# Low weights of the opening's features made on GpSimd instead of VectorE, and the first roots spread half a feature later

## The chip, the cores and the metric

The kernel runs on one core of a Trainium2 chip. The metric is the device time of one execution in microseconds (us), as the median of several runs; smaller is better. The engines are TensorE (PE in the profile), VectorE (DVE), ScalarE (ACT), GpSimd (POOL) and SyncE (SP, which here issues nearly all DMAs).

## The reference

One layer of a bidirectional encoder is applied to two groups of tokens, 2048 (prompt) and 512 (sample), each with the same 16 meta tokens ahead of them. All numbers are float32.

```python
u = rms_norm(h, norm_g)
proj = u @ w_in                                   # 1024 x 5376
qa, ka, va, za, qb, kb, vb, zb, ga, gb = jnp.split(proj, cuts, axis=-1)
o_a = neighbourhood_attention(qa, ka, va, na_rpb, n)      # 8 heads, 2-D windows
o_b = window_attention(qb, kb, vb, t5_bias, sink, n)      # 8 query heads, 2 key heads
y_a = (o_a * silu(za)) @ w_proj_a
y_b = (o_b * silu(zb)) @ w_proj_b
merged = sigmoid(ga) * y_a + sigmoid(gb) * y_b
out = rms_norm(h + merged @ w_out, final_g)               # meta tokens dropped
```

## The kernel before

The 2560 tokens are cut into five blocks of 512; the last block also carries the 16 meta tokens. The 5376 output columns of `w_in` are cut into 42 features of 128. Products are kept at float32 quality by splitting each operand into a high part (a cast, `fp32r`) and a low part (the rest): `project` computes a feature with `mm3`, three matmuls (L146: high weight by high input, L147: high by low, L148: low by high) for each of the 8 slices of the 1024 inputs, 24 matmuls of 512 columns in all. Key and value features of the last block are made in two column pieces, of 256 and of 272 columns, with 48 shorter matmuls.

`split_w` makes the two parts of one feature's weights, a tile `wt`, out of the raw tile `wraw` that a DMA brought. It works in two halves of 512 columns; each is a cast on ScalarE (L207) and a subtraction `l = r - h` (L208), on the engine that is handed in, or else on `lo_eng[0]`, which is VectorE until late in the program. There are two buffers each for `wraw` and `wt`: the cast of a feature's weights waits until TensorE has done the feature two before it, and the next raw DMA waits until a raw tile is split.

The change is in the opening, the first stage. `beside` computes 18 features of the last block (four of QA, four of QB, four of KA, four of VA, KB and VB), one after the other by `alone`, while the operands of blocks 0 and 1 are prepared by the steps of `prep_first` (L377 scaling, L445 to L461 sums and differences, L381 casts and L382 low parts). The roots of the last block's norm come from the generator `own` (`prep_last`): at the count `own[1][0]` of quarter features its sums run on TensorE (L360) and its reciprocal roots on VectorE (L153 to L163, and L177, which writes them on diagonals, `rs_dg`); at the last count of `own[1]` the roots are spread over the partitions by matmuls with ones (L185) and copied by ScalarE (L370). Until then the finished features wait in PSUM (`held[1]`), since their stores (L281: PSUM times root) need the roots.

After the 18 features comes the opening's exit. `begin` computes the first two products of blocks 0 and 1 (`pa`, `pc`, L850), and `sides_first` makes sums of the raw weights on VectorE (L816, L817, L821, L823: tiles `s`), which are split into the operands of the next products: `x2` (a tile `wt` made from `s`, used by the product called p6, `pa`, and by p5, `pe`) and `x3`, `x4` (used by p7 and later). `last_operands` makes eight more block operands at the same place (L381, L382). From there on TensorE goes through pairs of features.

TensorE and SyncE run in the order in which the code is written. The order of the other engines is set by a scheduler from its own estimates, so an edit can move their instructions elsewhere too; each engine then takes its instructions strictly in that order.

Of the kernel before, what the change touches and what calls it, by code (L numbers as in the profile page):

```python
# [95 lines left out]
def encoder_block(ctx: ExitStack, tc: tile.TileContext, xT, x_end, w_in, w_pa, w_pb, w_o, norm_g, final_g,  # L96
                  final_row, bias_a0, bias_a1, bias_a2, bias_a3, bias_b, bias_b0, outT_p, outT_s, out_e):
    nc = tc.nc
# [99 lines left out]
    def fetch_w(src):  # L198
        raw = wpool.tile([P, KT * P], F32, tag="wraw", name="wraw")
        if len(src.shape) == 3:  # L200
            move(raw.rearrange("p (a f) -> p a f", a=2), src.rearrange("a p f -> p a f"))
        else:
            move(raw, src)
        return raw

    def split_part(h, l, r, eng=None):
        nc.scalar.copy(h, r)  # L207
        low[0] = (eng or lo_eng[0]).tensor_sub(l, r, f32(h)).ins  # L208

    def split_w(raw, engines=()):  # L210

        wt = wpool.tile([P, 2, KT * P], F32R, tag="wt", name="wt")
        for i, c in enumerate(range(0, KT * P, 4 * P)):
            split_part(wt[:, 0, c : c + 4 * P], wt[:, 1, c : c + 4 * P], raw[:, c : c + 4 * P], *engines[i : i + 1])
        return wt

    class Weights:
# [16 lines left out]
        def next(self):  # L234
            i = self.i
            self.i += 1
            self.fetch(i + 2)
            self.split(i + 1)
            return self.wt.pop(i)
# [345 lines left out]
    def tick():  # L585
        for q in queue:
            q[0] -= 1
        due = [q for q in queue if q[0] <= 0]
        queue[:] = [q for q in queue if q[0] > 0]
        for _, fn, args in due:  # L590
            fn(*args)
# [243 lines left out]
    def sides_first(raws, x1):  # L835

        ss = [t[:, i] for t in (ev.tile([P, 2, WTOK], F32, tag="ev", name="s") for _ in range(2)) for i in range(2)]
        steps = sides(raws, x1, ss, nc.vector, None)
        next(steps)
        return steps  # L840
# [23 lines left out]
    def begin(f1, wa, x1, u, pool):  # L864

        a = bank("pa")
        product(a, x1[:, :, : 4 * P], u[0], True)
        s1 = snap(a, pool, "s1")
        c = bank("pc")
        product(c, x1[:, :, 4 * P :], u[1], True)  # L870
        store(f1, wa, c, (nc.vector.tensor_add, s1))
        return a
# [60 lines left out]
    def beside(fs, raws, wts, own, wa, steps, at, zeros=iter(())):  # L933

        held = [own, None if own is None else []]
        ws = [*fs, *both[0]]
        lag[0] = 4
        mark[0] = None  # L940
        at = list(at)
        q = 0
        for i, f in enumerate(fs):
            if i:
                wts.append(split_w(raws[i + 1]))
                if i + 3 < len(ws):
                    raws.append(fetch_w(w_in[ws[i + 3]]))
                next(zeros, None)
            for _ in alone(f, wts[i], held):
                q += 1  # L950
                if own is not None and q in own[1]:
                    next(own[0])
                    if q == own[1][-1]:
                        for fn in held[1]:
                            fn()
                        held[1] = None
                while at and at[0] <= q:
                    at.pop(0)
                    next(steps)
                tick()  # L960
        for r in steps:
            if r == "last":
                break
        first = sides_first(raws[-2:], wts[-1])
        raw1 = fetch_w(w_in[both[1][0]])
        a = begin(both[0][0], wa, wts[-1], us[wa], ev)
        with tc.issue_after(copied[0]):
            for _ in steps:
                pass
        return a, first, raw1  # L970
# [5 lines left out]
    firsts = [*range(QA, KA), *range(QB, KB), *range(KA, ZA), KB, VB]  # L976
# [19 lines left out]
    raws, wts = next(w0)  # L996
    own = prep_last(True)
    next(own)
    with tc.tile_pool(name="sp", bufs=1, reuse_waits="tile") as sp:
        loaded = []  # L1000
        steps = prep_first(sp, 0, loaded)
        next(w0)
        next(steps)
        next(w0)
        loaded.append(last_move[0])
        next(steps)
        zeros = zero_rows()
        next(zeros)
        begun = beside(firsts, raws, wts, (own, (9, 14)), 0, steps, [2, 20, 27, *(28 + 27 * i // 10 for i in range(16))],
                       zeros)  # L1010
    steps = [(0, 1), *((n, i) for n in range(1, KT) for i in (0, 1)), (KT, 0), (KT, 1), (KT, 2), (9, 1),
             *((j, i) for j in range(10, 18) for i in ((0, 2) if j % 2 == 0 else (1,)))]
    w0, opened = start_w(rest), []
    finals = pass_(0, *begun, prep_ahead(2), dict(zip(steps[:-1], steps[:-1])), lambda: opened.extend(next(w0)))
    raws, wts = opened
    next(w0)
    with tc.tile_pool(name="sp", bufs=1, reuse_waits="tile") as sp:
        steps = prep_second(sp, 2)
        next(steps)
        for fn in finals:  # L1020
            fn()
        next(w0)
        begun = beside(rest, raws, wts, None, 2, steps, range(1, 25, 3))
# [669 lines left out]
```

## Time and profile before

| | us |
|---|---|
| median of 3 runs | 1885.11 |
| lowest, highest | 1883.92, 1886.2 |
| profiled execution | 1884.6 |
| its span, first to last instruction | 1882.6 |
| TensorE busy | 1857.5 (99%) |
| VectorE busy | 1326.1 (70%) |
| ScalarE busy | 1144.5 (61%) |
| GpSimd busy | 729.2 (39%) |

The profiled execution is 0.5 us below the median. In the profile, a row of the timeline gives the start of an instruction (or a run of like ones, with their count), its length, engine, line, operation, what it writes and reads, and in brackets the idle time of that engine ahead of it with what ended it. Columns of a window are its bounds, length, busy time and instruction count, granted TensorE clock as a share of full speed, the DMA engines' share, and GB/s. The opening's 18 features run from about 7 us to 122 us of the span, and the exit from there to about 141 us.

### The profile page before, as it was taken

To read this page: it belongs to the slowest core of one execution; us is meant where nothing else is said; L and a number is where in the kernel's file an instruction comes from. 1 tells how busy PE (TensorE), PEld (TensorE's weight loads), DVE (VectorE), ACT (ScalarE), POOL (GpSimd) and SP (SyncE) were. 2 spreads that over 40 slices of the span, in tenths; PEclk is the share of its full clock that TensorE was granted. 3 is DMA by queue.
4 is the path that set the end of the run, shared out by engine and by line. 5 is a ranking of instruction groups with operands and counts; after the bars stand their busy time and mean duration, and the time that the engine had idled before them with its cause. 6 is when DMAs were issued, how large, how long until landed. Compare 5 with 4: busy or idle time off the path is not lost. (4 is left out here: it accounts for less than half of the span.)

```text
span 1882.6 us, 29816 instructions
## 1 busy us (share of the span) xinstructions
PE 1857.5 (99%) x9797; PEld 1585.1 (84%) x9797; DVE 1326.1 (70%) x2961; ACT 1144.5 (61%) x2528; POOL 729.2 (39%) x558
## 2 busy tenths in 40 slices
PE   8999999999999999999999999999999999999998
PEld 6988888888888888888888888888888888888887
DVE  8985667556477565544457888878887877888874
ACT  6444444434365444444456797797789778878932
POOL 2005343323203222322324435656744763685420
PEclk9999999999999999999999999999999999999999
DMA  7675666655295677644259878977986997697483
GB/s 262 199 195 183 194 184 182 209 188 179 84 341 185 189 216 199 208 139 160 104 187 316 274 221 265 305 213 249 319 275 187 316 307 227 218 315 259 118 301 133
DMA packets 288145, 414.35 MB, mean 220 GB/s; under 512 B 117736, under 2 KB 162360, under 8 KB 286456
## 3 DMA queue, kind: packets, MB, share of 16 engines
q1 hardware_dynamic: 287704, 412.45, 68.1%
q8 instruction: 78, 1.28, 0.3%
q14 instruction: 75, 0.61, 0.1%
q10 hardware_dynamic: 288, 0.01, 0.0%
HBM read 303.46 MB, written 108.91 MB: 219 GB/s over the span
## 5 line engine op out<-in xcount | busy, mean ns | idle before, releaser
L208 POOL TENSOR_TENSOR wt<-wraw,wt 128x512 fp32r<-128x512 f32 x164 | 213.0, 1317 | 266.9 <-ACT wt L207 266.8
L850 PE MATMUL pa<-u,wt 128*128 128x512 f32 x1008 | 244.5, 392 | 2.1 <-ACT wt L207 1.1
L850 PE MATMUL pa<-u,x 128*128 128x512 f32 x984 | 236.7, 389 | 0.4 <-ACT u L861 0.4
L850 PEld LDWEIGHTS pa<-u,wt 128*128 128x128 f32 x1008 | 189.9, 189 | 42.4 <-ACT wt L207 1.5
L207 ACT CAST wt<-wraw 128x512 fp32r<-128x512 f32 x312 | 178.0, 619 | 74.8 <-PE mm L148 29.8
L850 PEld LDWEIGHTS pa<-u,x 128*128 128x128 f32 x984 | 184.5, 188 | 39.2 <-ACT u L861 0.8
L821 POOL TENSOR_TENSOR s<-wraw,raw 128x512 f32<-128x512 f32 x40 | 58.2, 1456 | 279.4 <-DVE x L208 279.4
L146 PE MATMUL mm<-u,wt 128*128 128x512 f32 (+2 forms) x416 | 150.4, 362 | 7.1 <-ACT u L334 7.1
L816 POOL TENSOR_TENSOR s<-raw 128x512 f32<-128x512 f32 x40 | 58.1, 1454 | 232.8 <-DMA raw<-in_w_in_dram 116.0
L147 PE MATMUL mm<-u,wt 128*128 128x512 f32 (+2 forms) x416 | 146.8, 353 | 1.1 <-DVE u L335 1.1
L148 PE MATMUL mm<-u,wt 128*128 128x512 f32 (+2 forms) x416 | 146.6, 352 | 0.0
L208 DVE TENSOR_TENSOR wt<-wraw,wt 128x512 fp32r<-128x512 f32 x148 | 104.5, 744 | 52.3 <-ACT wt L207 52.1
L850 PE MATMUL pe<-u,wt 128*128 128x512 f32 x504 | 121.4, 390 | 0.0
L850 PE MATMUL pc<-u,wt 128*128 128x512 f32 x504 | 121.1, 389 | 0.0
L850 PE MATMUL pe<-u,x 128*128 128x512 f32 x480 | 115.3, 389 | 0.0
L850 PEld LDWEIGHTS pe<-u,wt 128*128 128x128 f32 x504 | 94.6, 188 | 19.6
L850 PEld LDWEIGHTS pc<-u,wt 128*128 128x128 f32 x504 | 94.6, 188 | 19.6
L1145 DVE TENSOR_TENSOR pl<-tp,ph 128x384 fp32r<-128x384 f32 (+6 forms) x160 | 94.9, 593 | 20.9 <-ACT ph L1144 18.7
L1144 ACT CAST ph<-tp 128x384 fp32r<-128x384 f32 (+6 forms) x160 | 81.5, 510 | 43.0 <-PE tp L1141 41.4
L146 PE MATMUL pso<-mh,wt 128*128 128x512 f32 x256 | 107.1, 418 | 0.0
L829 POOL TENSOR_TENSOR s<-wraw,s 128x512 f32<-128x512 f32 x40 | 54.0, 1350 | 136.3 <-DVE wt L208 136.3
L850 PEld LDWEIGHTS pe<-u,x 128*128 128x128 f32 x480 | 90.1, 188 | 18.7
(258 smaller groups left out, 5024.8 us busy)
## 6 DMA issues: line engine op xcount, KB each, us to landing
wraw<-in_w_in_dram SPq DMA_DIRECT2D x86, 512.0 KB
raw<-in_w_in_dram SPq DMA_DIRECT2D x40, 512.0 KB
q<-qa SPq DMA_DIRECT2D x40, 512.0 KB
wraw<-in_w_o_dram SPq DMA_DIRECT2D x32, 512.0 KB
kbt<-kb SPq DMA_DIRECT2D x32, 384.0 KB
qa<-evq SPq DMA_DIRECT2D x20, 512.0 KB
qb<-evq SPq DMA_DIRECT2D x20, 512.0 KB
ka<-evk SPq DMA_DIRECT2D x20, 512.0 KB
```

What stands on the lines that cost most here:

```text
L146: nc.tensor.matmul(ps, wh, uh, start=first, stop=False)
L147: nc.tensor.matmul(ps, wh, ul, start=False, stop=False)
L148: nc.tensor.matmul(ps, wl, uh, start=False, stop=last)
L207: nc.scalar.copy(h, r)
L208: low[0] = (eng or lo_eng[0]).tensor_sub(l, r, f32(h)).ins
L816: eng.tensor_add(s1, a21, a22)
L821: eng.tensor_sub(s3, a11, a21)
L829: eng.tensor_sub(s4, a12, s2)
L850: nc.tensor.matmul(ps, wt[:, a, s], u[:, b, kk, :], start=first and kk == 0 and i == 0, stop=kk == 3 and i == 2, skip_group_check=True)
L1144: nc.scalar.copy(ph_[:kb, a], tb)
L1145: nc.vector.tensor_sub(pl_[:kb, a], tb, f32(ph_[:kb, a]))
```

## The change

From the third feature on, `split_w` in the first call of `beside` is handed engines for its subtractions. For the weights split during features three and four (counted from one) the second half goes to GpSimd and the first stays on VectorE; from feature five on both halves go to GpSimd. The second call of `beside` (blocks 2 and 3) has no `own` and stays as it was. The last count of `own` goes from 14 to 16, so that the roots are spread after the fourth feature instead of in its middle.

```diff
         for i, f in enumerate(fs):
             if i:
-                wts.append(split_w(raws[i + 1]))
+                wts.append(split_w(raws[i + 1], (nc.vector if i < 4 else nc.gpsimd, nc.gpsimd) if own is not None and i > 1
+                                   else ()))
...
-        begun = beside(firsts, raws, wts, (own, (9, 14)), 0, steps, [2, 20, 27, *(28 + 27 * i // 10 for i in range(16))],
+        begun = beside(firsts, raws, wts, (own, (9, 16)), 0, steps, [2, 20, 27, *(28 + 27 * i // 10 for i in range(16))],
```

In what follows the lines are those of the kernel before; behind the edit the changed file has one line more. On TensorE the spread (L185, five matmuls) stood behind the first 12 matmuls of the fourth feature and now stands behind all 24; nothing else of TensorE's order changes, and SyncE's order is the same.

GpSimd, from its first sums (`rsp`, the squares of block 1) to its first work for the pairs (L816, L817); rows with - are of before, with + of now:

```order
 L420 TENSOR_TENSOR rsp_349<-sq 128x512
-L423 TENSOR_TENSOR rsp_349<-rsp_349,sq 128x512 x6
+L423 TENSOR_TENSOR rsp_349<-rsp_349,sq 128x512 x2
+L208 TENSOR_TENSOR wt<-wraw,wt 128x512
+L423 TENSOR_TENSOR rsp_349<-rsp_349,sq 128x512 x4
+L208 TENSOR_TENSOR wt<-wraw,wt 128x512 x29
 L816 TENSOR_TENSOR s_1747<-raw_1697 128x512
 L817 TENSOR_TENSOR s_1748<-s_1747,wraw 128x512
```

Thirty subtractions came to a queue that was empty between the sums and the pairs; the same thirty are gone from VectorE's queue.

ScalarE during the key features (features 9 to 12): `wt` is a feature's weights, `u` an operand of blocks 0 and 1, `evk` and `km` belong to the stores. Before:

```order
L207 CAST wt<-wraw 128x512 x2
L381 CAST u_748<-tt 128x512
L256 ACTIVATE evk<-tkv 128x512
L381 CAST u_750<-x_350 128x512
L256 ACTIVATE km<-tm 128x48
L207 CAST wt<-wraw 128x512 x2
L381 CAST u_751<-x_352 128x512
```

and now:

```order
L381 CAST u_748<-tt 128x512
L207 CAST wt<-wraw 128x512 x2
L256 ACTIVATE evk<-tkv 128x512
L256 ACTIVATE km<-tm 128x48
L381 CAST u_750<-x_350 128x512
L381 CAST u_749<-x_351 128x512
L381 CAST u_752<-tt 128x512
L381 CAST u_751<-x_352 128x512
L207 CAST wt<-wraw 128x512 x2
```

The casts of the block operands, which wait for VectorE, moved ahead of the casts of the weights.

ScalarE at the exit, where `wt<-s` are the two halves of `x2`, `s_1640` is the copy of the first product out of PSUM, and the `u` are those of `last_operands`:

```order
-L207 CAST wt<-s 128x512
+L207 CAST wt<-s 128x512 x2
 L861 COPY s_1640<-pa 128x512
 L381 CAST u_1661<-x_352 128x512 x4
-L381 CAST u_1670<-x_353 128x512
-L207 CAST wt<-s 128x512
-L381 CAST u_1670<-x_353 128x512 x3
+L381 CAST u_1670<-x_353 128x512 x4
 L253 CAST evq<-tq 128x8x4x16
```

The second half of `x2` moved ahead of the copy and of five casts of `u`.

VectorE at the same place now; before, the second of the two L208 stood behind the L281 and five of the eight L382, and the sums L816, L821 and L817 behind the last L281 of the features:

```order
L281 TENSOR_TENSOR tkv<-mm,rs_294 128x256
L816 TENSOR_TENSOR s<-wraw 128x512
L821 TENSOR_TENSOR s<-wraw 128x512
L817 TENSOR_TENSOR s<-s,wraw 128x512
L281 TENSOR_TENSOR tkv<-mm,rs_294 128x256
L792 TENSOR_TENSOR tm<-mm,rs_294 128x16
L208 TENSOR_TENSOR wt<-s,wt 128x512
L823 TENSOR_TENSOR s<-wraw,s 128x512
L208 TENSOR_TENSOR wt<-s,wt 128x512
L382 TENSOR_TENSOR u_1661<-x_352,u_1661 128x512 x3
```

Both subtractions of `x2` moved ahead of the operands of `last_operands`.

## The prediction

> **What bounds the kernel.** I read the page first, then the list of TensorE's waits, then the timeline of the opening engine by engine.
>
> ```profile
> PE 1857.5 (99%) x9797; PEld 1585.1 (84%) x9797; DVE 1326.1 (70%) x2961; ACT 1144.5 (61%) x2528; POOL 729.2 (39%) x558
> PE mm L146 <- ACT u L334: 7.1, 1, 7.1
> ...
> PE pa L850 <- ACT wt L207: 1.1, 1, 1.1
> ...
> PE rs_rb L185 <- DVE rs_dg L177: 1.0, 1, 1.0
> PE pa L850 <- DVE wt L208: 1.0, 1, 1.0
> ```
>
> TensorE is the bound: it is busy for 99% of the span, so VectorE's 70% buys nothing by being lower. The change can win only where TensorE waits, or runs at a lower clock, in or right behind the opening. The list has three such places: the roots (1.0), and two waits at the exit for the weights `x2` (1.1 and 1.0). The 7.1 us are the start of the program, which the edit doesn't reach.
>
> **The roots.**
>
> ```profile
> 30.01 1.74 DVE L177 TENSOR_TENSOR rs_dg<-ident,rs 128x512 f32<-128x512 f32 x2
> 31.72 1.48 PE L185 MATMUL rs_rb<-rs_dg,ones 128*128 128x128 f32 x10 [1.02 <-DVE rs_dg L177]
> ```
>
> The spread waits 1.02 us for the diagonals, done at 31.75. Placed 12 matmuls later it would come up at 31.72 - 1.02 + 2.76 = 33.46 us (12 matmuls take 2.76, from the rows of the exit below), 1.7 us after the diagonals. VectorE also has one subtraction less ahead of the roots. So the wait goes: -1.0 us. Its ends are 0 and -1.0. What is late next: the stores of the first features start about 1.5 us later, but they wait in PSUM, and five banks hold features one to five.
>
> **The exit.** Here the gain is larger than the two waits.
>
> ```profile
> 122.38 2.92 PE L850 MATMUL pa<-u,wt 128*128 128x512 f32 x12
> 125.14 2.88 PE L850 MATMUL pc<-u,wt 128*128 128x512 f32 x12
> 129.09 0.73 PE L850 MATMUL pa<-u,wt 128*128 128x512 f32 x2 [1.07 <-ACT wt L207]
> 130.82 4.14 PE L850 MATMUL pa<-u,wt 128*128 128x512 f32 x10 [1.00 <-DVE wt L208]
> 134.81 2.91 PE L850 MATMUL pe<-u,wt 128*128 128x512 f32 x12
> ...
> 131.00:133.00 2.00, 2.00 (x6) 0.58 0.35 143
> ...
> 123.77 0.63 ACT L207 CAST wt<-s 128x512 fp32r<-128x512 f32 x1 [3.81 <-DVE s L816]
> ...
> 125.82 2.70 ACT L381 CAST u<-x 128x512 fp32r<-128x512 f32 x5
> 128.42 0.62 ACT L207 CAST wt<-s 128x512 fp32r<-128x512 f32 x1
> ...
> 130.09 0.68 DVE L208 TENSOR_TENSOR wt<-s,wt 128x512 fp32r<-128x512 f32 x1
> ```
>
> A product of 12 matmuls takes 125.14 - 122.38 = 2.76 us. The third should start at 125.14 + 2.76 = 127.90 and the fourth at 130.66; it starts at 134.81, 4.15 us late. Of these, 2.07 are waits, and the rest is the clock: it was granted at 0.58 right behind the waits (the window's fifth column), and ten matmuls took 3.99 us instead of 2.30. The first wait is for a cast that stands behind five casts of `u`, the second for a subtraction at 130.09 that stands behind operands too. In the new order both casts of `x2` stand ahead of the copy of `pa`, and both subtractions right behind the last store. They need the last feature done at 122.4, two casts and some 2 us of VectorE: ready at about 125, needed at 127.9. So this delay should go whole, as long as VectorE is no more than some 3 us behind: -4.2 us, with 0 as the other end.
>
> **What the thirty subtractions cost.** The two engines don't run side by side freely. Where GpSimd worked next to VectorE, later in the same opening:
>
> ```profile
> L208 POOL TENSOR_TENSOR wt<-wraw,wt 128x512 fp32r<-128x512 f32 x164 | 213.0, 1317 | 266.9 <-ACT wt L207 266.8
> ...
> 141.43 1.75 POOL L821 TENSOR_TENSOR s<-wraw,raw 128x512 f32<-128x512 f32 x1
> 143.14 1.74 POOL L829 TENSOR_TENSOR s<-wraw,s 128x512 f32<-128x512 f32 x1
> ...
> 141.95 0.68 DVE L281 TENSOR_TENSOR tq<-pe,u 128x512 f32<-128x512 f32 x1
> 142.55 1.18 DVE L208 TENSOR_TENSOR wt<-s,wt 128x512 fp32r<-128x512 f32 x1
> 143.66 1.78 DVE L254 TENSOR_TENSOR evq<-tq,evq 128x512 fp32r<-128x512 f32 x1
> 145.36 1.77 DVE L208 TENSOR_TENSOR x<-s,x 128x512 fp32r<-128x512 f32 x1
> ```
>
> VectorE's instructions with both inputs in SBUF (L208, L254) take up to 1.78 us; L281, with one input in PSUM, keeps its 0.68. They alternate: one on each engine per 1.7 us (143.66 to 145.36). Alone on VectorE such an instruction follows the next in 0.60 (two L208 in 70.86 to 72.07, below). So a subtraction on GpSimd holds VectorE for up to 1.7 - 0.6 = 1.1 us, where on VectorE it cost 0.60: moving it can cost VectorE 0.5 us rather than save 0.6.
>
> The Trainium skill says so too (SBUF — State Buffer, "Who interferes with whom"): GpSimd and a VectorE instruction with two SBUF inputs exclude each other for the whole instruction. This trace agrees on the kind. Where that page of the Trainium skill would charge a hold at its whole length, the 1.3 us that GpSimd's own L208 take in the mean (1317 ns, first row), the rows show 1.1; by its reading the sum below would be 4 us longer.
>
> Is there room for it?
>
> ```profile
> 61.78:122.58 60.80, 57.09 (x117) 1.00 0.63 179
> 61.78:122.58 60.80, 13.35 (x21) 0.00 (x0) 1.00 0.63 179
> ...
> 67.55 1.14 ACT L207 CAST wt<-wraw 128x512 fp32r<-128x512 f32 x2 [1.64 <-PE mm L148]
> 73.42 1.14 ACT L207 CAST wt<-wraw 128x512 fp32r<-128x512 f32 x2 [3.08 <-PE mm L148]
> ...
> 70.86 1.28 DVE L208 TENSOR_TENSOR wt<-wraw,wt 128x512 fp32r<-128x512 f32 x2
> 72.07 0.68 DVE L461 TENSOR_TENSOR x<-x,tt 128x512 f32<-128x512 f32 x1
> ...
> 73.72 0.68 DVE L445 TENSOR_TENSOR tt<-x,x 128x512 f32<-128x512 f32 x1
> ...
> L281 DVE TENSOR_TENSOR tkv<-mm,rs 128x256 f32<-128x256 f32 x19 | 7.9, 416 | 1.8 <-PE mm L148 1.8
> ```
>
> The first window is VectorE alone, the second the L208 in it (21, of which one began in the stretch before); the last row is a group of that window. In features 9 to 18 VectorE is busy 57.1 of 60.8 us. Twenty subtractions at 0.60 leave, 57.1 - 12.0 = 45.1, and twenty holds at 1.1 come, 22.0: 67.1 us of work in 60.8, 6.3 too many if no hold is hidden. Instructions that read PSUM run beside a hold: the 19 L281 above are 7.9 us, and with L792 and the copies of V about 11, one fifth of the work. If holds are hidden in that share the sum is 62.7, 1.9 too many. So VectorE falls 2 to 6 us behind by the end of the opening, most of it in the key features, where it had no idle time at all.
>
> Lag alone doesn't stop TensorE, since PSUM has room for some features' results. It reaches TensorE through ScalarE, whose weight casts now stand behind casts of operands that wait for VectorE. A feature lasts 73.42 - 67.55 = 5.87 us. From its cast the weights need 0.5 for the first half and 1.7 for a GpSimd instruction that alternates, 2.2 in all, before the next feature's third matmul; so the cast may be 3.6 us late. Before, the L445 of feature 10 ended at 74.4; in the new order such an L445 and a cast of `u` stand ahead of a weight cast due at 73.4, which makes 1.5 us. Each key feature adds (22.0 - 12.0)/10 = 1.0 at most. After two or three features the 3.6 are used up, about at features 12 and 13: a wait between 0 and 3 us. I take 1.2, nearer the low end, because before the ninth feature VectorE has slack again and later features carry less work.
>
> One more thing is late behind the exit. SyncE's raw weights for the next pair stand behind the stores of the last V feature:
>
> ```profile
> 118.71 3.16 SPq L142 DMA_DIRECT2D va<-vn  x4
> ...
> 127.67 0.46 SPq L142 DMA_DIRECT2D wraw<-in_w_in_dram  x1
> ...
> 54.23 0.62 SPq L142 DMA_DIRECT2D wraw<-in_w_in_dram  x1
> ...
> 59.05 0.62 ACT L207 CAST wt<-wraw 128x512 fp32r<-128x512 f32 x1 [3.26 <-DMA wraw<-in_w_in_dram]
> ...
> 140.88 1.30 PE L850 MATMUL pa<-u,wt 128*128 128x512 f32 x5
> ```
>
> SyncE issues without a break from 118.71 to 127.67, so if the V copies come 1 to 4 us later (their ScalarE cast now stands behind a weight cast, and VectorE lags), the raw weights are issued that much later. A raw tile took 59.05 - 54.23 = 4.8 us from issue to use; so it comes at 133.5 to 136.5 and its low half a good 1 us behind. TensorE wants it at 140.88, or at 136.7 with the exit's 4.15 us gone: a wait of 0 to 1.5 us. I take 0.7.
>
> At nothing I cost: the subtractions of features four and five (a half each, while GpSimd waits for squares and the stores are held anyway), those of features six to eight (VectorE waits for the roots of blocks 0 and 1 there), and everything behind the first pair, whose order on TensorE is unchanged. If VectorE were full there too, each hold would cost its 0.5.
>
> **The sum.** Roots -1.0, exit -4.2, casts in the key features +1.2, raw weights +0.7: -3.3 us. The profiled execution took 1884.6 (span 1882.6 and 2.0 around it), so 1881.3; the median of the runs stands 0.5 above it, so 1881.8. All terms at their best give -5.2, which is 1879.9. About 0.2% (3.8 us) is what a measurement of this kernel can tell from no change, that is 1881.3 to 1888.9.
>
> **The rivals.**
>
> *All of it is hidden.* The lag stays under the slack of 3.6 us and the raw weights come in time: -5.2 us, 1879.9. For it speaks that a fifth of VectorE's work reads PSUM, and that the low parts no longer queue behind VectorE's rest: before, the subtraction began at 70.86 for a cast begun at 67.55. Against it speaks that VectorE has no idle time in the key features and that every hold there has to be paid.
>
> *VectorE's lag eats most of it.* The holds are hidden little, the casts wait 3 us in all, and VectorE comes to the exit about 4 us behind, so that the subtraction of `x2` is late again and half of the exit's delay stays: -1.0 - 2.1 + 3.0 + 0.7 = +0.6 or, with less lag, -2: 1883 to 1886.
>
> *Slower, with the lag at full size.* All holds cost 1.1, so VectorE is 6.3 us behind. From 3.6 on TensorE is paced by it: 2.7 us of wait, and by the exit's rows, where 2.07 us of wait brought 10 matmuls from 2.30 to 3.99, the clock drops once in the features too: +1.7. At the exit the lag leaves the delay in place, 0 instead of -4.2, and the raw weights cost 1.5: -1.0 + 2.7 + 1.7 + 1.5 = +4.9, so 1890. It decides once the lag at feature 13 is above some 5 us. The Trainium skill leans to this side (Perfetto Trace Analysis, "Optimizing Scalar/DVE Operations"): work moved from VectorE to GpSimd might not help, as they share a read port. The rows of 141 to 147 us agree; that VectorE is full in this stretch is what would make it count.
>
> *The exit's wait is not the order's.* If the order on ScalarE and VectorE mattered less than some DMA, only the roots would be gained: 1884. The two releasers are named by the list as ScalarE's cast and VectorE's subtraction, so I give this little.
>
> **How the numbers follow.** The forecast (a net gain between 1.5 and 4.5, that is 1880.6 to 1883.6) 0.46; all hidden 0.21; lag eats most 0.17; slower 0.12; exit unchanged 0.04. Faster by over 0.2% needs below 1881.3: all of the hidden case and two fifths of the forecast, 0.40. Slower by over 0.2% is the slower case less its mild part and some mishap of it: 0.11. The rest, 0.49, is within. The range leaves out the slower case and the edge of the best: 1879.5 to 1887.5; the cases within it are of both signs, and the likeliest one's own range is 1880.6 to 1883.6.
>
> **What would show it.** Right: no wait of L185 for `rs_dg`; the fourth product of the exit starts 2.76 us behind the third, at a clock of 1.00; VectorE's L382, L377 and L257 in features 9 to 13 with lengths near 1.8 us; GpSimd's thirty L208 at 1.3 to 1.75; ScalarE's weight casts in features 10 to 13 ended by VectorE instead of by TensorE. Wrong: TensorE waits of over 3 us in total between 60 and 122 us, a window there with a clock under 0.9, or `x2` late once more at the exit. If the holds are much shorter than 1.1 us the gain is larger than I say.

## The result, and the profile after

The changed kernel is slower: 1891.8 us in the median of five runs (1889.69 to 1894.34), against 1885.11 before; the ratio is 1.0037, with an interval of 1.0023 to 1.0051. Forecast were 1881.8 us, and 1887.5 as the upper end. A second measurement (e12 below) gave 1.0044, 1.0031 to 1.0058.

The profiled execution took 1894.34 us (span 1892.6), the slowest of the five. First the busy times, then the list of TensorE's waits between 40 and 150 us (columns: who waited for what, us in all, times, the longest):

```profile
PE 1860.9 (98%) x9797; PEld 1586.5 (84%) x9797; DVE 1326.7 (70%) x2931; ACT 1143.8 (60%) x2528; POOL 776.9 (41%) x588
...
PE mm L148 <- POOL wt L208: 2.7, 2, 1.9
PE pa L850 <- ACT s L861: 0.6, 1, 0.6
PE pa L850 <- DVE wt L208: 0.3, 1, 0.3
PE fin_v L428 <- DVE rsp L423: 0.3, 1, 0.3
```

VectorE has 30 instructions less (2961 to 2931) and is just as busy: 1326.7 us against 1326.1. The subtractions are gone from it, and their time is not. The wait of the roots (L185 for `rs_dg`) is gone, as forecast. The exit's two waits for `x2` (1.1 and 1.0) have shrunk to 0.6, now for the copy of `pa` (L861), and 0.3. New are two waits for GpSimd's low weights. The longer one, on TensorE, ScalarE, GpSimd and VectorE:

```profile
81.76 0.28 PE L147 MATMUL mm<-u,wt 128*128 128x256 f32 x1
83.94 0.40 PE L148 MATMUL mm<-u,wt 128*128 128x256 f32 x1 [1.89 <-POOL wt L208]
...
79.58 0.62 ACT L381 CAST u<-tt 128x512 fp32r<-128x512 f32 x1 [1.96 <-DVE tt L445]
80.10 1.14 ACT L207 CAST wt<-wraw 128x512 fp32r<-128x512 f32 x2
...
80.80 4.32 POOL L208 TENSOR_TENSOR wt<-wraw,wt 128x512 fp32r<-128x512 f32 x2 [4.86 <-ACT wt L207]
...
80.87 0.68 DVE L382 TENSOR_TENSOR u<-tt,u 128x512 fp32r<-128x512 f32 x1
81.47 0.68 DVE L450 TENSOR_TENSOR x<-x,x 128x512 f32<-128x512 f32 x1
82.08 0.68 DVE L257 SCALAR_TENSOR_TENSOR evk<-tkv,evk 128x512 fp32r<-128x512 f32 x1
82.81 1.14 DVE L257 SCALAR_TENSOR_TENSOR km<-tm,km 128x48 fp32r<-128x48 f32 x1
83.87 1.80 DVE L382 TENSOR_TENSOR u<-x,u 128x512 fp32r<-128x512 f32 x1
```

It reads as a chain. ScalarE stood 1.96 us idle ahead of a cast of `u` that needed VectorE's L445, so the cast of the weights began at 80.10. GpSimd began at 80.80, and its two subtractions took 4.32 us together, the first of them 3.09 (to 83.88, by the single records; 3.09 again in e12). In that time VectorE ran three instructions with two SBUF inputs at their full speed of 0.68 us. GpSimd came through only in the gap ahead of L257 of `km`, which had to wait for ScalarE. TensorE started 0.06 us after GpSimd's first half. The shorter wait (0.83 us, over at 63.90) begins with a DMA: the cast of those weights waited for its raw tile until 61.65, in before until 59.05. Behind the longer wait the clock dropped (columns: window, length, TensorE's busy time and count, granted clock, DMA share, GB/s):

```profile
80.00:85.00 5.00, 3.11 (x23) 0.92 0.91 300
85.00:90.00 5.00, 5.00 (x33) 0.74 0.49 145
```

33 matmuls in 5 us stand where before had 43. The exit's rows, to be set beside those of before:

```profile
128.63 2.91 PE L850 MATMUL pa<-u,wt 128*128 128x512 f32 x12
131.39 2.88 PE L850 MATMUL pc<-u,wt 128*128 128x512 f32 x12
134.88 0.73 PE L850 MATMUL pa<-u,wt 128*128 128x512 f32 x2 [0.61 <-ACT s L861]
135.96 2.56 PE L850 MATMUL pa<-u,wt 128*128 128x512 f32 x10 [0.35 <-DVE wt L208]
138.35 2.88 PE L850 MATMUL pe<-u,wt 128*128 128x512 f32 x12
...
142.58 2.56 PE L850 MATMUL pa<-u,x 128*128 128x512 f32 x10 [0.24 <-DVE x L208]
```

From the first product to the fourth it takes 138.35 - 128.63 = 9.72 us, where before took 12.43 and three products without a stop take 8.28. So the exit did gain 2.7 us. It began 6.25 us later than before's, so that its fourth product still starts 3.5 us late.

A last loss is far behind the change. By the first matmuls of like pieces of work, the changed kernel stands 4.1 us behind before at 200 to 720 us, 3.2 at 1320 us, and 9.9 from 1540 us to the end. No engine's order differs between 1320 and 1540 us. TensorE's waits from 1310 to 1540 us, of before first:

```profile
PE tp L1141 <- DVE pr L1065: 2.9, 4, 1.9
...
PE tp L1142 <- DVE pr L1066: 7.2, 4, 3.0
PE s L1118 <- DMA kd<-ka: 1.3, 1, 1.3
```

### The profile page after: what moved, and what is told of

It is laid out like the page before. It is cut to its first block, busy times and chain, and to the rows that moved or that the text cites. A ratio compares the mean times of both kernels' runs of the same rounds, so it can differ in the third digit from the quotient of the medians.

```text
span 1892.6 us, 29838 instructions
## 1 busy us (share of the span) xinstructions
PE 1860.9 (98%) x9797; PEld 1586.5 (84%) x9797; DVE 1326.7 (70%) x2931; ACT 1143.8 (60%) x2528; POOL 776.9 (41%) x588
## 4 chain that ended last, share of the span: by engine, by line
PE 80%; DVE 6%; DMA 6%; ACT 4%; issue 2%; SPq 1%; POOL 1%; ACTq 0%; DVEq 0%
PE pa L850 23%; PE pe L850 11%; PE pc L850 6%; PE tp L1142 3%; PE pso L148 2%; PE pso L146 2%; PE pso L147 2%; PE mm L147 2%; PE mm L146 2%; PE mm L148 2%; PE psa L146 2%; PE tp L1244 2%; PE psa L148 2%; PE psa L147 2%; PE psb L148 1%
## 5 line engine op out<-in xcount | busy, mean ns | idle before, releaser
L208 POOL TENSOR_TENSOR wt<-wraw,wt 128x512 fp32r<-128x512 f32 x194 | 259.8, 1357 | 317.3 <-ACT wt L207 317.2
L821 POOL TENSOR_TENSOR s<-wraw,raw 128x512 f32<-128x512 f32 x40 | 58.2, 1456 | 273.8 <-DVE x L208 273.8
L146 PE MATMUL mm<-u,wt 128*128 128x512 f32 (+2 forms) x416 | 151.7, 365 | 7.4 <-ACT u L334 7.4
L148 PE MATMUL mm<-u,wt 128*128 128x512 f32 (+2 forms) x416 | 148.4, 357 | 2.7 <-POOL wt L208 2.7
L147 PE MATMUL mm<-u,wt 128*128 128x512 f32 (+2 forms) x416 | 148.2, 356 | 0.8 <-DVE u L335 0.8
L816 POOL TENSOR_TENSOR s<-raw 128x512 f32<-128x512 f32 x40 | 60.4, 1509 | 148.3 <-DMA raw<-in_w_in_dram 145.9
L208 DVE TENSOR_TENSOR wt<-wraw,wt 128x512 fp32r<-128x512 f32 x118 | 86.5, 771 | 49.1 <-ACT wt L207 49.1
L1055 ACT ACTIVATE s<-s,nm 128x384 f32<-128x384 f32 (+5 forms) x160 | 87.1, 545 | 35.4 <-DVE nm L1048 34.3
L1145 ACT CAST ph<-tp 128x384 fp32r<-128x384 f32 (+6 forms) x160 | 81.5, 509 | 43.1 <-PE tp L1142 41.6
```

The lines of the kernel that those rows point to most:

```text
L146: nc.tensor.matmul(ps, wh, uh, start=first, stop=False)
L147: nc.tensor.matmul(ps, wh, ul, start=False, stop=False)
L148: nc.tensor.matmul(ps, wl, uh, start=False, stop=last)
L816: eng.tensor_add(s1, a21, a22)
L821: eng.tensor_sub(s3, a11, a21)
L1055: nc.scalar.activation(out, s, AF.Exp, bias=nm, scale=-1.0, accum_out=sm)
```

## The experiments

There are two theories for the opening's loss. Theory 1: GpSimd's subtractions hold VectorE back, and VectorE drags along what waits for it. Theory 2: what costs is only that a low weight comes later from GpSimd than from VectorE. Theory 3, a side line: the later spread and its later stores do it. All edits are to the kernel before, unless another is named; times are medians, with the ratio to before on the same chip. Before's own medians differ by up to 1.7 us from chip to chip, so a difference between kernels on different chips is good to about that.

| kernel | us | before there | ratio, 95% interval |
|---|---|---|---|
| e1 later spread alone | 1884.11 | 1885.62 | 0.9988 (0.9980 to 0.9997) |
| e2 GpSimd's low weights alone | 1892.31 | 1885.62 | 1.0034 (1.0022 to 1.0047) |
| e3 spread, 8 early low weights | 1889.45 | 1885.62 | 1.0017 (1.0006 to 1.0029) |
| e4 order of the exit alone | 1882.74 | 1885.62 | 0.9985 (0.9976 to 0.9994) |
| e5 spread and exit | 1880.58 | 1884.60 | 0.9974 (0.9964 to 0.9984) |
| e6 e5, subtractions made twice | 1903.65 | 1884.60 | 1.0095 (1.0082 to 1.0108) |
| e8 e5, low weights copied | 1888.63 | 1884.60 | 1.0013 (1.0004 to 1.0023) |
| e9 e5, 8 early low weights | 1881.43 | 1884.60 | 0.9982 (0.9972 to 0.9992) |
| e10 e5, second halves only | 1888.44 | 1885.78 | 1.0013 (1.0005 to 1.0022) |
| e7 e5, 22 late low weights | 1890.86 | 1885.78 | 1.0018 (1.0008 to 1.0029) |
| delay of 3.2 us | 1889.98 | 1885.78 | 1.0021 (1.0010 to 1.0031) |
| e12 the changed kernel again | 1894.56 | 1886.30 | 1.0044 (1.0031 to 1.0058) |
| e13 delay of 4.1 us | 1888.44 | 1885.06 | 1.0020 (1.0010 to 1.0029) |
| e14 delay of 8.2 us | 1893.88 | 1885.06 | 1.0050 (1.0035 to 1.0064) |
| e15 e5, delay of 9.1 us | 1891.26 | 1885.06 | 1.0031 (1.0019 to 1.0043) |
| e16 e5, 30 fills and a tile | 1887.17 | 1884.74 | 1.0016 (1.0007 to 1.0025) |
| e17 e5, 60 fills and a tile | 1887.61 | 1884.74 | 1.0017 (1.0008 to 1.0026) |
| e18 e5, 30 fills, no tile | 1881.17 | 1885.12 | 0.9985 (0.9976 to 0.9994) |

**The two parts, one at a time.** e1 changes `(own, (9, 14))` to `(own, (9, 16))` and nothing else:

> Before, with the later spread alone: (9, 16) in place of (9, 14); all lows of the opening on VectorE as before. Theory 1 (GpSimd's subtractions hold VectorE back, VectorE drags ScalarE's casts, TensorE then waits and loses its clock) and theory 2 (only the longer subtraction itself, 1.3 against 0.6 us, makes weights late): this part has no GpSimd subtraction, so nothing is lost; 1884.0 to 1885.5 us, TensorE's wait at the second sums gone, first matmul of the exit (pa) between 128.0 and 129.5 us where before has 129.09. Theory 3 (the later spread moves the 14 kept stores and with them the raw weights' DMAs by 2 to 3 us, and these make the casts late): most of the loss is here, 1887 to 1890 us, pa of the exit at 131 us or later.

It gained 0.12% (0.03 to 0.20), 1.5 us in the medians, and the second sums (L428) started at 40.42 instead of 41.44. Theory 3 falls.

e2 is the other part:

```diff
-                wts.append(split_w(raws[i + 1]))
+                wts.append(split_w(raws[i + 1], (nc.vector if i < 4 else nc.gpsimd, nc.gpsimd) if own is not None and i > 1 else ()))
```

> Before, with GpSimd's low weights alone; the spread at (9, 14) as before. Theories 1 and 2: the loss of the whole change and the roots' 1 us not gained, 1890 to 1893 us; a TensorE wait of 1 to 2 us on a GpSimd low weight between 75 and 90 us with a clock under 0.9 behind it, pa of the exit at 133 us or later. Theory 3: 1884 to 1887 us, pa of the exit by 131 us.

It has the whole loss, 6.7 us, and the two waits for GpSimd (2.7 us in all, the longest 1.9). One thing was expected and didn't come: the clock stayed at 1.00 from 80 to 90 us, and the opening lost no less without the drop: the exit's fourth product starts at 140.56, 5.7 us behind before's (3.5 in the change).

**The exit's order.** In before, ScalarE casts five pieces of `u` ahead of the second half of the weights `x2`. e4 makes `last_operands` stand behind the cast and the subtraction that belong to the third product:

```diff
     def split_part(h, l, r, eng=None):
-        nc.scalar.copy(h, r)
-        low[0] = (eng or lo_eng[0]).tensor_sub(l, r, f32(h)).ins
+        made.append(nc.scalar.copy(h, r).ins)
+        made.append((eng or lo_eng[0]).tensor_sub(l, r, f32(h)).ins); low[0] = made[-1]
...
-        first = sides_first(raws[-2:], wts[-1])
+        first, x2 = sides_first(raws[-2:], wts[-1]), made[-4:-2] if own is not None else 2 * [copied[0]]
...
-        with tc.issue_after(copied[0]):
+        with tc.issue_after(copied[0]), tc.issue_after(x2[0]), tc.issue_after(x2[1]):
```

> Before, with only the order of ScalarE and VectorE at the exit changed: the casts and subtractions of the weights of the exit's third product stand ahead of the casts and subtractions that make the operands u5 and u6, as in the changed kernel, with no GpSimd subtraction and the spread where it was. If the prediction's exit term is right (2.07 us of waits and 2.1 us of half clock before pe, all of it gone): 1880.5 to 1882 us, pe of the exit 9.3 us behind pa's first matmul less 3.5 to 4.2, no clock under 0.9 there. If u5 and u6 are then late instead: 1884 to 1886 us, with the wait at the products of u5 and u6. If the changed kernel lost its exit's gain again (it started pe 3.47 us behind pa where before took 5.72): gain of 2.2 to 3, 1882 to 1883.

```profile
123.55 2.91 PE L850 MATMUL pa<-u,wt 128*128 128x512 f32 x12
126.30 2.88 PE L850 MATMUL pc<-u,wt 128*128 128x512 f32 x12
129.02 2.88 PE L850 MATMUL pa<-u,wt 128*128 128x512 f32 x12
131.74 2.88 PE L850 MATMUL pe<-u,wt 128*128 128x512 f32 x12
```

TensorE's rows of e4 have no wait left and no half clock. From the first product to the fourth it is 8.19 us instead of 12.43: 4.24 gained, the forecast's 4.2. Some of it went again ahead of the exit, where the last feature ended 1.2 us later than before's; in the medians 2.9 us are left.

e5 is e4 with the later spread:

> The two parts that gained when made alone, together: the exit's third product's weights cast and subtracted ahead of u5 and u6, and the spread at (9, 16); no low weight on GpSimd. Measured alone they gave 2.9 and 1.5 us in the medians. If they add up: 1880 to 1882 us, pe of the exit 3.2 to 4.2 us ahead of before's. If the later spread only moves a wait that the exit then hides or returns: 1882 to 1884.

The gains add up: 1880.58 us, 4.0 under before on its chip, and the fastest of all. There is no TensorE wait in its list between 40 and 150 us, and VectorE makes every low weight of the opening. Its fourth product of the exit:

```profile
129.72 2.88 PE L850 MATMUL pe<-u,wt 128*128 128x512 f32 x12
```

So the change's two good effects don't need GpSimd, and against e5 the thirty subtractions cost 1891.8 - 1880.6 = 11.2 us.

**A few low weights.** e3 is the change with `1 < i < 7` in place of `i > 1` (8 subtractions, before the key features):

> The change with GpSimd making low weights for the features before the key features only (8 of its 30 subtractions); the later spread kept. Theory 1: VectorE lags where its two-input work stands beside GpSimd's, in the key features, so nothing is lost: 1883.5 to 1885.5 us. Theory 2: each GpSimd subtraction adds its 0.7 us alike, so 8 of 30 cost 8/30 of 6.7 us, and with the roots' gain 1885.5 to 1887. Theory 3: 1888 to 1892.

It lost more than theory 1 or 2 said. Its time lies where theory 3 had put it, but the reason is another, which the rows of its exit show:

```profile
131.30 0.73 PE L850 MATMUL pa<-u,wt 128*128 128x512 f32 x2 [2.63 <-ACT wt L207]
133.28 4.15 PE L850 MATMUL pa<-u,wt 128*128 128x512 f32 x10 [1.25 <-DVE wt L208]
...
126.47 4.26 ACT L381 CAST u<-x 128x512 fp32r<-128x512 f32 x8
130.63 0.61 ACT L207 CAST wt<-s 128x512 fp32r<-128x512 f32 x1
```

Here all eight casts of `u` stand ahead of that weight cast (before: five, the change: none). ScalarE's order at the exit moves with any edit ahead of it. e9 is e5 with the same eight subtractions and so with the exit's order fixed:

> Against e5: GpSimd makes the 8 low weights of the features before the key features. The same 8 with the old exit order gave 1889.45, where the second half of the exit's weights was cast behind all eight casts of u5 and u6 (before: behind five). If that order was the loss: within 1.0 us of e5. If the 8 subtractions cost by themselves (vt of the sixteenth feature came 1.3 us later than with the later spread alone): 1.0 to 2.0 us above e5.

0.9 us over e5 in the medians (1.9 at the exit's fourth product, 131.59 against 129.72): the first eight cost little, and most of e3's loss was the order.

**Hold or lateness.** e6 leaves every low weight to VectorE, as in e5, and lets GpSimd make 28 of them once more, behind VectorE, into the raw tile that nobody reads again:

```diff
-        made.append((eng or lo_eng[0]).tensor_sub(l, r, f32(h)).ins); low[0] = made[-1]
+        made.append((eng if eng is nc.vector else lo_eng[0]).tensor_sub(l, r, f32(h)).ins); low[0] = made[-1]; (eng is nc.gpsimd and eng.tensor_sub(r, r, f32(h)))
```

> Against e5: VectorE makes every low weight as before, and behind 28 of them, at the places of the change, GpSimd makes the same subtraction once more into the raw weights, which nobody reads again. GpSimd's presence without its latency. Theory 1 (GpSimd's two-input subtractions hold VectorE's two-input instructions back): VectorE falls behind as in the change or more, since it keeps its own subtractions; 1885 to 1889 us, TensorE waits for VectorE or for casts that VectorE delayed between 55 and 100 us, vt of the sixteenth feature 3 us or more behind e5's. Theory 2 (the weights were late only by the length of GpSimd's subtraction): the weights are as early as in e5; within 1.0 us of e5.

23.1 us over e5, far more than the 1885 to 1889 us expected, and all of it in the opening (23.1 at the exit's fourth product). TensorE's waits in e6 all lead to VectorE:

```profile
PE mm L148 <- DVE wt L208: 6.7, 7, 2.7
PE fin_v L428 <- DVE rsp L423: 3.1, 1, 3.1
PE vt L638 <- DVE vn L254: 2.9, 1, 2.9
```

From the start of a weight cast to VectorE's subtraction it took 4.3 to 6.3 us from 70 to 105 us; in e5 it took 0.7 to 4.0 there. So GpSimd's presence stops TensorE. Something else is in it too: the second subtraction keeps the raw tile, SyncE waited 21.5 us in all for it before it could issue the next raw weights, and casts came later by that. And it is a harsher case than the change, since VectorE keeps its own 0.6 us for each as well.

e8 is the reverse: VectorE subtracts into the raw tile, and GpSimd copies that into the low weight, with one SBUF input (`eng.tensor_copy(l, r)`).

> Against e5: at the same 28 places VectorE subtracts into the raw weights and GpSimd copies the result into the low weights, with one input of SBUF in place of two. Latency without (or with less of) the hold: a low weight comes a whole GpSimd copy, about 0.7 to 1.5 us, later than in e5. Theory 1, if a copy holds VectorE less than a subtraction: VectorE's two-input instructions of the key features stay near 0.68 us, and the time is within 1.5 us of e5. Theory 2: 4 to 7 us above e5, with TensorE waiting for GpSimd at the third matmul of a feature's first tile (1 to 2 us each).

VectorE was held much less: its groups from 60 to 100 us are 3.2 us longer than e5's for their counts, 0.27 for each of 12 copies (L382 at 748 ns, before 682, the change 1415). Still the time is 8.0 us over e5, 6.9 of it by the exit's fourth product (136.63), with TensorE waiting for GpSimd:

```profile
L382 DVE TENSOR_TENSOR u<-x,u 128x512 fp32r<-128x512 f32 x6 | 4.5, 748 | 0.0
...
PE mm L148 <- POOL wt L208: 3.1, 3, 1.4
PE fin_v L428 <- DVE rsp L423: 1.2, 1, 1.2
```

So theory 1 alone falls too: with little of the hold left, lateness still costs. Not all of the 6.9 us is lateness, though: the wait of L428 ends with VectorE, and the clock stood at 0.91 from 40 to 60 us. In e10 the lateness is taken away instead: VectorE makes the first halves, GpSimd only the second, which TensorE wants half a feature later (`nc.vector, nc.gpsimd` for `i > 1`).

> Against e5 (1880.6): from the third feature on VectorE makes the low weights of the first half of a feature, GpSimd those of the second half, which TensorE needs half a feature (2.8 us) later: 16 subtractions on GpSimd in place of the change's 30. If the lateness of the low weights is what TensorE pays (GpSimd's 1.7 us for a half, behind a cast that comes late), it is hidden here: within 1.5 us of e5, no TensorE wait on a GpSimd low weight over 0.5 us. If VectorE's held time is what counts whatever the place: 16/30 of the 11.2 us by which the change stands above e5, so 1885 to 1888 us.

No wait for GpSimd is left, and the time is still 7.9 us over e5, 5.8 of it by the exit's fourth product (135.51). The longest wait that came is a hold, on GpSimd, VectorE and in the list of TensorE's waits:

```profile
66.95 1.77 POOL L208 TENSOR_TENSOR wt<-wraw,wt 128x512 fp32r<-128x512 f32 x1 [3.58 <-DVE tt L454]
...
67.51 1.76 DVE L382 TENSOR_TENSOR u<-x,u 128x512 fp32r<-128x512 f32 x1
69.20 0.68 DVE L208 TENSOR_TENSOR wt<-wraw,wt 128x512 fp32r<-128x512 f32 x1
...
PE mm L148 <- DVE wt L208: 1.8, 1, 1.8
```

VectorE's L382 took 1.76 us beside GpSimd's subtraction, and the first half of the next weights stood behind it. So theory 2 alone falls. Each effect costs some 6 to 7 us by the exit where little or nothing of the other is left. The change has both (8.6 by the exit), and how much of that is the one's and how much the other's these runs don't divide.

e7 gives GpSimd the 22 low weights from the eighth feature on (`i > 6`):

> Against e5: GpSimd makes the 22 low weights from the eighth feature on, the key features among them; the 8 before are VectorE's. The 8 alone cost 0.9 us. If the loss lies in the key features, where VectorE has no idle time (60 to 95 us): 1888 to 1891.5 us, TensorE waiting 2 us or more in all for GpSimd's low weights. If the 30 subtractions cost alike: 22/30 of 11.2, so 1888 to 1889, the waits spread evenly. If the loss needs both (the early ones shift what the later ones meet): under 1886.

10.3 us over e5, with one wait of 1.9 us for GpSimd and the clock at 0.91 from 80 to 100 us. The 8 early ones cost 0.9 us (e9) and these 22 cost 10.3: the loss lies in the key features and behind them.

**The loss behind 1320 us.** First whether a shift alone causes it, with 14 matmuls more in the fifth pair:

```diff
-            e = bank("pe")
+            e = bank("pe"); [nc.tensor.matmul(e, x["p5"][:, 0, :P], u[3][:, 0, 0, :], start=True, stop=False, skip_group_check=True) for _ in range(14 if wa == 0 and j == 4 else 0)]
```

> Before, with 14 more 128x512 matmuls on TensorE in the fifth pair (their sum is overwritten): a plain delay of 14 x 0.23 = 3.2 us at about 170 us, before anything waits for memory, and nothing else changed. It asks whether the late part of the program (1320 to 1530 us, where the DMA engines are full) turns a shift of 3 us into more, as the profiled execution of the changed kernel had it (3.2 us behind at 1318 us, 10 at 1525). If the shift is passed on as it is: 3.2 us over before, 1887.5 to 1889. If the late part adds to any shift: 1890 to 1894. If it is swallowed there: under 1886.5.

3.2 us put in, 4.2 measured. The changed kernel once more:

> The changed kernel itself once more, on this chip and in more executions. Its profiled execution lost 3.2 to 4 us by the end of the opening and 6.7 us more between 1320 and 1530 us, where no engine's order had changed, and its five times were 6.7 us above before in the median. The plain delay of 3.2 us came out as 4.2, with times spread over 8 us. If the late 3 us were those five executions' own: 3 to 5 us over before. If the changed kernel meets the late part worse by itself: 6 to 8 us over before again, and its profile again gains 3 us or more behind before between 1320 and 1530 us.

8.3 us over before on its chip, and its profile again gains between 1320 and 1540 us: from 4.0 to 9.4 us behind. So that loss is the kernel's, not one execution's. In this profile the same wait of 1.9 us for GpSimd left the clock at 1.00:

```profile
80.00:85.00 5.00, 3.10 (x25) 2.89 (x25) 5.00 (x7) 2.23 (x5) 4.33 (x2) 1.00 0.87 284
85.00:90.00 5.00, 4.98 (x41) 4.77 (x39) 4.96 (x9) 3.83 (x8) 2.27 (x2) 1.00 0.35 105
```

e13 and e14 are the delay with 18 and 36 matmuls, e15 is e5 with 40:

> Before with a plain delay of 18 x 0.23 = 4.1 us in the fifth pair, which is how far the changed kernel stood behind before at 720 us in both of its profiles (4.1 and 4.6), and nothing else changed. The changed kernel added 5.4 and 6.7 us between 1320 and 1530 us in those profiles. If a shift of this size by itself is what the late, DMA-full part turns into more: 1891 to 1894.5 us, and the profile adds 4 us or more behind 1320 us. If the late loss belongs to the changed kernel in another way than by its shift: 1889 to 1890.5, the profile adding 2 us or less there, as the delay of 3.2 us did (1.7).

> The same with 36 matmuls, 8.2 us. If the late part adds in proportion to the shift (1.7 on 2.65 measured, so 0.6 of it): 5 us more, 1898 to 1900 us. If it adds 0 to 2 us whatever the shift: 1893.5 to 1896. If it works by the phase of the time, any addition from 0 to 6 us could come, without order between 14, 18 and 36 matmuls.

> e5 (exit and roots, no low weight on GpSimd) with 40 matmuls of delay, 9.1 us, which puts it 4.0 us behind before at 720 us, where the changed kernel stands, by another opening. e5 measured 1880.6 and added nothing in the late part. If the late loss goes with the shift against the clock time at which the late part is entered: 1880.6 + 9.1 + 4 to 6, so 1893.5 to 1896. If it belongs to the low weights on GpSimd: 1889 to 1891, the profile adding 2 us or less behind 1320 us.

4.1 us put in came out as 3.4, 8.2 as 8.8, and 9.1 as 10.7. Their profiles add -0.4, 1.4 and 2.5 us behind 1320 us. A shift is passed on about as it is; it is not the cause. e16 and e17 were to test the number of GpSimd's instructions, with small fills at the program's start:

> e5 (exit and roots, no low weight on GpSimd; 1880.6 us) with 30 small fills (128x8) on GpSimd at the start of the program, where it has nothing to do: as many more instructions on GpSimd as the changed kernel has, without their length and their holds. Behind 1320 us the profiles of kernels with 0 or 8 more GpSimd subtractions added -0.4 to 2.5 us, with 16 2.8, with 22 3.2, with 28 2.3 and 5.1, with 30 5.4 to 6.7. If the mere number of instructions in GpSimd's stream (where its code is loaded in pieces) is what the late part feels: 1883.5 to 1887 us, 4 us or more of it behind 1320 us. If not: 1879.5 to 1882, with 2.5 us or less added there.

> The same with 60 fills. By the number of instructions: another late addition than with 30, 1880 to 1892 us. If the number doesn't matter: 1879.5 to 1882.5, as e5.

They lost 6.6 and 7.0 us to e5, but not late. The fills wrote into a new tile of 32 bytes (`wpool.tile([P, 8], ...)`), and TensorE's matmuls of the pairs grew longer, with no wait. The groups of e5 and then of e16:

```profile
L850 PE MATMUL pa<-u,x 128*128 128x512 f32 x984 | 236.7, 389 | 1.0 <-ACT u L861 1.0
L850 PE MATMUL pe<-u,x 128*128 128x512 f32 x480 | 115.3, 389 | 0.0
...
L850 PE MATMUL pa<-u,x 128*128 128x512 f32 x984 | 239.8, 392 | 0.0
L850 PE MATMUL pe<-u,x 128*128 128x512 f32 x480 | 118.4, 396 | 0.0
```

So they say nothing of the late part, and e18 puts the fills into the tile of `ident` ahead of its making:

> e5 with 30 small fills on GpSimd at the start of the program, this time into the tile that the identity is then made in, so that no tile is added and none moves (in e16 and e17 a tile of 32 bytes was added and TensorE's matmuls of the pairs came 0.228 us apart in the mean in place of 0.226, from 200 to 480 us on; their time says nothing of the late part). If the number of instructions on GpSimd matters to the late part: 1884 to 1887 us, 4 us or more of it behind 1320 us. If not: 1879.5 to 1882, with 2.5 us or less added there.

0.6 us over e5, with 0.8 added late: the number of instructions is not the cause either. What is left is an association. Behind 1320 us the profiles of kernels with 16 to 30 low weights on GpSimd, made or copied there, added 2.3 to 6.7 us (e2, e6, e7, e8, e10, the change twice), those with none or 8, the two with the extra tile aside, -0.4 to 2.5. The two ranges touch. Two more signs go with it. From 1320 to 1540 us VectorE waited for the DMA of `ba` (the bias that L1047 adds) for 3.6 to 4.3 us in the three profiles with all thirty (the change twice and e2), for 0.2 in before and for 2.3 at most in any other. And the clock stood at 0.99 there in e2, e6, e7, e8, e10 and e12, and at 1.00 in every kernel with none or 8, but also in the change's first profile. No run shows the way from the low weights to these; that stays open.

## Why the prediction was wrong

**Roots: right, and in one execution lost again.** The wait went, and e1 gained 1.5 us in the medians for the 1.0 forecast. In the changed kernel TensorE then met 16 small matmuls (L428) behind a wait of 0.3 us. In the first profile the clock was granted at 0.90 from 40 to 44 us and at 0.67 from 44 to 48, and the matmuls from 43.1 to 46.5 came 0.43 apart instead of 0.23, which cost about 1.6 us; in e12 it stayed at 1.00 behind the same wait. The prediction had no term for that.

**Exit: right for the order, and a third of it lost.** -4.2 forecast, 4.24 in e4 with the order alone. In the changed kernel 2.7 of it were kept. The rest went by raw weights: VectorE's first sum for `x2` (L816) began at 131.79, behind a wait of 1.43 us for a raw tile that SyncE had issued at 128.05, right behind 5.9 us of stores of a V feature (in e5 it was issued at 117.40). So the casts of `x2` began at 132.59 and 133.72, the copy of `pa` behind them at 134.24 and the second low half at 135.22, and TensorE waited for both. In e12 VectorE's wait for that tile is 1.75 us, in e10 1.85. "`x2` late once more at the exit" was one of the signs against the forecast, and it came.

**The subtractions: the term that failed.** +1.2 us, 0 to 3, stood for the key features, and the work of all thirty has cost 11.2 us against e5, about 8.6 of it by the exit (fourth product at 138.35 against 129.72). By the same matmuls the change is 2.1 us behind e5 at 60 us, 3.4 behind the ninth feature, 7.1 behind the twelfth and still at the exit's first product, and 8.6 at its fourth; in e12, where the clock never fell in the opening, 0.5, 2.6, 4.8, 6.0 and 8.0. The size of the hold was right. VectorE's groups from 60 to 100 us, before and after, with GpSimd's:

```profile
L208 DVE TENSOR_TENSOR wt<-wraw,wt 128x512 fp32r<-128x512 f32 x16 | 10.4, 683 | 0.6 <-ACT wt L207 0.5
L382 DVE TENSOR_TENSOR u<-x,u 128x512 fp32r<-128x512 f32 x9 | 6.1, 682 | 0.0
L257 DVE SCALAR_TENSOR_TENSOR km<-tm,km 128x48 fp32r<-128x48 f32 x4 | 0.8, 199 | 0.0
L461 DVE TENSOR_TENSOR x<-x,tt 128x512 f32<-128x512 f32 x2 | 1.4, 682 | 0.0
...
L382 DVE TENSOR_TENSOR u<-x,u 128x512 fp32r<-128x512 f32 x6 | 8.5, 1415 | 0.0
L461 DVE TENSOR_TENSOR x<-x,tt 128x512 f32<-128x512 f32 x2 | 3.3, 1662 | 0.1
L257 DVE SCALAR_TENSOR_TENSOR km<-tm,km 128x48 fp32r<-128x48 f32 x4 | 2.8, 706 | 0.1
...
L208 POOL TENSOR_TENSOR wt<-wraw,wt 128x512 fp32r<-128x512 f32 x12 | 19.9, 1675 | 18.9 <-ACT wt L207 18.9
```

The groups of L382, L461 and L257 (`km`) alone grew by 4.4, 1.9 and 2.0 us for their counts; with the smaller ones (L257 of `evk`, L450, L454, L254) it is 11.6 us for 12 subtractions on GpSimd, 0.97 each, where 1.1 was assumed. L377, for which the prediction expected lengths near 1.8 us too, stayed at 0.74 in the mean. The 11.6 us are as much as VectorE got rid of in this stretch (its 16 L208, 10.4 us), which is why its busy time stayed. The Trainium skill (SBUF — State Buffer, "SBUF: two separate sides") states that of a GpSimd instruction that reads SBUF and a VectorE instruction with two SBUF inputs the one that starts first has the shared ports for its whole instruction. These rows agree that VectorE waits, 0.97 us for each in the mean; but at 80.80 GpSimd's recorded start stands 0.07 us ahead of L382's, and it was GpSimd that waited.

What failed is the step from there to TensorE, "the cast may be 3.6 us late". It gave GpSimd 1.7 us for an instruction that alternates. At 80.80 it took 3.09, kept out by three instructions of VectorE in a row; no row of before showed a GpSimd subtraction against a full stream of VectorE's. The low half was due at 82.05 (83.94 less the wait of 1.89), so by the prediction's 2.2 us its cast had to begin by 79.85. It began at 80.10, 0.25 late, in feature 12, where the forecast had put the end of the slack. GpSimd then began 0.2 us later than allowed for and took 1.39 more: that is the wait. So the lag of the cast was about right, and GpSimd's length was not. The other wait, 0.8 us at the start of the ninth feature, came with weights split in the eighth, where the prediction had costed nothing. And the clock's price, 1.7 us (of 5 us at 0.92 and 5 at 0.74), stood only in the rival.

On the clock, the Trainium skill (TensorE: Matmul & The Clock Gate, "Part 1: The HAM clock gate") states an idle window of some 3.4 us behind which the clock halves. Here a shorter wait, of 1.9 us, was followed by 0.74 in one execution and by 1.00 in two others (e2, e12), and e2 lost no less. So the clock is not what decides the result.

**Raw weights behind the exit: the size by luck.** +0.7 forecast; from the fourth product to the product that needs them (140.88 in before, 144.98 now) it is 6.63 us instead of 6.07, so 0.56 more. But TensorE's wait in there is the 0.24 us at 142.58, for VectorE's low part of `x` (L208). These raw weights stopped nothing, neither here nor in e5, where the exit's 4.2 us are gone. What the term describes, raw weights late behind the stores of V features, did happen, one tile earlier and at the exit itself, as said above.

**Everything behind the first pair at nothing: wrong**, by 3 to 5 us in the medians (6.7 and 8.3 us, of which some 4 stand at 720 us). Its cause is not found.

The rival "slower, with the lag at full size" had 1890 us and named a good part of it: a wait of 2.7 (2.7 came), a clock drop of 1.7 (1.7 in one execution). It was wrong that none of the exit's gain is kept, and it too had nothing behind the first pair, so that it comes so near to 1891.8 is in part luck. Of the signs against the forecast, "TensorE waits of over 3 us in total between 60 and 122 us" was just missed with 2.7; a clock under 0.9 came in one execution, and `x2` late at the exit in both.

## What to carry to other kernels

Moving a two-input subtraction from VectorE to GpSimd relieves VectorE of nothing while VectorE has two-input work queued: here each cost it 0.97 us for the 0.68 saved. Price such a move from the stretch where it stands, both ways: what VectorE loses, and how long GpSimd waits for a gap in VectorE's stream (here up to 3.1 us for 1.3). And when an edit shifts a scheduler's order somewhere else, make that shift alone first: here it was the gain (e5, 1880.58 us), and the edit itself only loss.

## What was not expected of the hardware

- With a tile of 32 bytes in each partition more in a pool (e16, e17), matmuls that read other tiles were longer: 396 ns instead of 389 for one group of 480, 392 instead of 389 for one of 984. By the busy times of the two groups that is 3.1 us each. That the tiles' places do it is the likely reading, since the same 30 fills without a new tile (e18) did not; it is not shown, and which place is bad wasn't tried.
- A stream of VectorE instructions kept a waiting GpSimd subtraction out for three instructions, and a GpSimd subtraction held even a VectorE instruction of 48 columns (L257 of `km`) to 706 ns in the mean, from 199.
- Plain delays of 3.2, 4.1, 8.2 and 9.1 us came out as 4.2, 3.4, 8.8 and 10.7: in this kernel a shift at about 170 us reaches the end nearly whole.
